# A hold and a pin for the conditioning passes around the column change of the first down product

## The chip, the cores and the metric

The kernel runs on one core of one Trainium2 chip. The metric is the device time of one execution in microseconds (us). A core has five engines with a queue of instructions each: PE (matmuls, with PEld for its weight loads), DVE and ACT (elementwise work), POOL, and SP, which here only issues DMAs. Each engine takes its own instructions in the order in which they stand, and an instruction waits there until the semaphores that it needs have been raised by other engines or by a landed DMA.

## What is computed

One layer of a decoder at batch 1, 256 positions and width 2048, all in fp32. Nine vectors of 2048 numbers, the conditioning, come from one vector `c`:

```python
mod = (silu(c) @ w_ada + b_ada).reshape(b, 9, 2048)
h = modulate(rms_norm(x, norm_ffn1), mod[0], mod[1])
x = x + 0.5 * mod[2] * swiglu(h, w_ffn1_gu, w_ffn1_down)     # DFF = 5632
h = modulate(rms_norm(x, norm_mix), mod[3], mod[4])
x = x + mod[5] * token_mixing(h, w_in, w_ret_branch, w_swa_branch, w_out, sinks)
h = modulate(rms_norm(x, norm_ffn2), mod[6], mod[7])
x = x + 0.5 * mod[8] * swiglu(h, w_ffn2_gu, w_ffn2_down)
return rms_norm(x, norm_final)
```

`w_ada` has 2048 x 18432 numbers. It is applied to a single row, so the kernel does that product on DVE, not on PE.

## The kernel before

**Matmuls in three parts.** A product in fp32 precision is made of three passes in the faster format fp32r. Each operand is split in a high part (a cast) and a low part (what the cast lost); then high by high, low by high and high by low are added up in PSUM (lines 338, 339 and 341 in `products`). A weight tile `raw` is 128 x 4 x 512 numbers, 1 MB, and comes in by one DMA from SP (`load`, line 328). It is used in two halves; a **half step** is one of them: ACT casts the high part `wh` (line 351), DVE subtracts to get the low part `wl` (line 353), and PE runs 12 matmuls, two k blocks by two row tiles by three. The left operand of a down product, the activations, is split in the same way on ACT and DVE (`a`, lines 386 and 387). There are four buffers for `raw`, and three each for `wh` and `wl`.

**The down product** (`down_product`) multiplies the 256 x 5632 activations with `w_ffn1_down`, 2048 columns wide. It does columns 0 to 1023 first: 11 blocks of k, each a `gemm_part` with two weight tiles, so four half steps a block. The results of the four PSUM banks are then multiplied with the gate row and added to `x` on DVE (`add_gated`, lines 607 and 608), with a sum of squares on ACT (line 536). Then columns 1024 to 2047 follow into the same four banks: seven blocks in the same way, and the last four in an order written out by hand. Going from the first two column groups to the last two is the **column change**.

**The conditioning passes.** While the first feed-forward part runs, the vectors 2, 4 and 3 of the conditioning are made beside it. A row tile of `w_ada` (128 x 2048, 1 MB) is loaded by SP (`ada_load`, line 201) and reduced against `silu(c)` on DVE in four passes of 512 columns (`ada_pass`, line 206; in the trace each is a pass and a short read of its sum). The generator `conditioning` yields after each pass. `tick` is called after each half step; it adds `rate` to a count and takes one pass for each whole number reached. When it takes a pass, the generator first issues the load of the row tile after the next boundary (`ahead`, four passes on). The row tiles live in two places, halves of one `slot` tile (`two_rows`), so the load of a row tile waits until the last pass of the row tile two before it is done.

**What sets the order.** SP's queue stands in the order in which the program is written. The orders of PE, DVE and ACT are made by the scheduler of the framework, which may pull an instruction ahead of its place in the program; `tc.issue_after(x)` forbids that it goes ahead of `x`. `low[-1]` is the newest low part made by `split`. Only the last part of a down product has an order written out by hand.

Of the kernel before, what the change touches and what calls it, by code (L numbers as in the profile page):

```python
# [21 lines left out]
NT = S // P  # L22
KD = D // P
KF = DFF // P
CH = 512
KB = 4
# [51 lines left out]
def layer_kernel(  # L78
# [40 lines left out]
    def nm(s):  # L119
        uid[0] += 1  # L120
        return f"{s}_{uid[0]}"

    def acc_bank():
        return psa.tile([P, CH], F32, tag="acc", name=nm("pa"))
# [70 lines left out]
    AQ = 4  # L195

    def ada_load(m, k, w, loads=1):
        src = w_ada[(m * KD + k) * P : (m * KD + k + 1) * P, :]
        for i in range(loads):
            at = slice(i * D // loads, (i + 1) * D // loads)  # L200
            nc.sync.dma_start(w[:, at], src[:, at])

    def ada_pass(k, w, sums, q, passes=AQ):

        at = slice(q * D // passes, (q + 1) * D // passes)
        nc.vector.tensor_tensor_reduce(  # L206
            out=w[:, at],
            in0=w[:, at],
            in1=cact[:, at],
            scale=1.0,  # L210
            scalar=0.0,
            op0=ALU.mult,
            op1=ALU.add,
            accum_out=sums[:, k, q : q + 1],
        )

    def ada_sums():
        return two.tile([P, KD, AQ], F32, tag="sums", name=nm("sums"))

    def ada_end(m, ks, sums, i=None, passes=AQ):  # L220

        dest = modc[:, m, ks]
        nc.vector.tensor_reduce(out=dest, in_=sums[:, ks, :passes], axis=AX.X, op=ALU.add)
        nc.vector.tensor_add(dest, dest, bcols[:, m, ks])
        if i is not None:
            nc.vector.tensor_mul(dest, dest, gains[:, i, ks])
# [16 lines left out]
    def conditioning(outputs, place, behind):  # L243


        tiles = [(m, k) for m, _, _ in outputs for k in range(KD)]
        held = {}
        step = 0
        for m, gain, row in outputs:
            sums = ada_sums()  # L250
            for k in range(KD):
                for q in range(AQ):
                    for i in range(step // AQ, min((step + pace["ahead"]) // AQ + 1, len(tiles))):
                        if i not in held:
                            held[i] = place()
                            ada_load(*tiles[i], held[i])
                    if behind is not None and step < 2 * AQ:
                        with tc.issue_after(behind.ins):
                            ada_pass(k, held[step // AQ], sums, q)
                    else:  # L260
                        ada_pass(k, held[step // AQ], sums, q)
                    step += 1
                    if k == KD - 1 and q == AQ - 1:
                        ada_end(m, slice(0, KD), sums, gain)
                        if row is not None:
                            gate_out(m, row)
                    yield
# [15 lines left out]
        return nc.gpsimd.dma_start(row, gate_d[m // 3][None, :].broadcast_to([P, D]))  # L283


    pace = {"steps": iter(()), "rate": 0.0, "due": 0.0, "behind": None}

    def set_pace(outputs, halves, place, ahead):
        assert next(pace["steps"], None) is None
# [3 lines left out]
        pace["ahead"] = ahead  # L293

    def tick():
        pace["due"] += pace["rate"]
        while pace["due"] >= 1.0:
            pace["due"] -= 1.0
            next(pace["steps"], None)
# [16 lines left out]
    def step():  # L316

        while side:
            try:
                next(side[0])  # L320
                break
            except StopIteration:
                side.pop(0)
# [33 lines left out]
    cast, low, newest = [], [], []  # L357
# [32 lines left out]
    def gemm_part(act, w, col0s, banks, kb, KT, ahead=None):  # L390

        pairs = [act.pair(kb * 2 + h) for h in range(2)]
        for i, c0 in enumerate(col0s):
            raw = None if ahead else load(w, kb, c0)
            for h in range(2):
                if ahead:
                    wh, wl = ahead[h]
                else:
                    wh, wl = split(wsp, "w", raw[:, 2 * h : 2 * h + 2, :], CH)
                ah, al = pairs[h]  # L400
                products(
                    banks[i], ah, al, wh, wl, kb + h == 0, kb * KB + 2 * h + 2 == KT
                )
                tick()
            turn_step()

    def gemm(act, w, col0s, KT=KD, ahead=None):
        banks = [[acc_bank() for _ in range(NT)] for _ in col0s]
        for kb in range(KT // KB):
            gemm_part(act, w, col0s, banks, kb, KT, None if kb else ahead)  # L410
            step()
        return banks
# [286 lines left out]
    def down_product(act, w, gate, KT, spare, before, after):  # L699


        ssq = small(NT * 4, "ssq")
        banks = gemm(act, w, [0, CH], KT=KT)
        for i in range(2):
            for t in range(NT):
                add_gated(banks[i][t], t, i * CH, gate, ssq)
        c0s = [2 * CH, 3 * CH]
        banks = [[acc_bank() for _ in range(NT)] for _ in c0s]
        nb = KT // KB
        for kb in range(nb - 4):  # L710
            gemm_part(act, w, c0s, banks, kb, KT)
        with tc.manual_schedule(engines=ORDERED):
            a, b = nb - 2, nb - 1
            home = home_tile().rearrange("p i (h n) -> p (i h) n", h=2)
            pairs, late = {}, {}

            def place(kb, h):
                if kb >= a:
                    halves = home[:, (kb - a) * 2 + h].rearrange("p (i n) -> p i n", i=2)
                    return [halves[:, i] for i in range(2)]  # L720
                if kb == a - 1:
                    return None
                return [back.tile([P, CH], F32R, tag="back", name=nm("back")) for _ in range(2)]

            for kb in (a - 2, a - 1, a, b):
                wt = weight(w, kb, c0s[0])
                pairs[kb] = []
                for h in range(2):
                    pairs[kb].append(act.pair(kb * 2 + h, place(kb, h)))
                    products(  # L730
                        banks[0], *pairs[kb][h], *wt(h), kb + h == 0, kb == b and h == 1
                    )
                n = {a - 2: a - 2, a - 1: a, a: b, b: a - 1}[kb]
                wt = weight(
                    w, n, c0s[1], spare if n == a - 2 else None if n < a else home_views()
                )
                late[n] = [(n, h, wt(h)) for h in range(2)]
            steps = [step for kb in (a - 2, a, a - 1, b) for step in late[kb]]

            def last(t, which):  # L740
                for kb, h, (wh, wl) in which:
                    products(
                        banks[1], *pairs[kb][h], wh, wl, kb + h == 0, kb == b and h == 1, [t]
                    )

            last(0, steps)
            before()
            root_table()
            for t in range(NT):
                add_gated(banks[0][t], t, c0s[0], gate, ssq)  # L750
            c0, y = c0s[1], {}

            def gated(t):
                y[t] = t512()
                nc.vector.tensor_mul(y[t], banks[1][t], gate[:, c0 : c0 + CH])

            def added(t):
                xs = x_sb[:, t, c0 : c0 + CH]
                nc.vector.tensor_add(xs, xs, y[t])

            def squared(t):
                square_sum(
                    ssq[:, t * 4 + 3 : t * 4 + 4], x_sb[:, t, c0 : c0 + CH], flat_tile
                )

            after(
                [Root(ssq, t) for t in range(NT)],
                (gated, added, squared),
                [lambda i=i: last(1, steps[i : i + 1]) for i in range(8)],
            )  # L770
# [113 lines left out]
    held = Held()  # L884
# [5 lines left out]
    behind = [[back.tile([P, CH], F32, tag="back", name=nm("back")) for _ in range(NT)] for _ in range(2)]  # L890
# [15 lines left out]
    def place(m, k):  # L906
        if k < 1:
            rows_of[m, k] = raw_row()
        else:
            ring.append(ring.pop(0))  # L910
            rows_of[m, k] = ring[-1]
        ada_load(m, k, rows_of[m, k], 2 if k < 2 else 1)
# [45 lines left out]
    banks, moved = {}, set()  # L958
# [50 lines left out]
    for g, ks in enumerate(groups):  # L1009
# [5 lines left out]
        due = 0 if final else 2 * len(groups[g + 1])  # L1015
# [21 lines left out]
    gate = gate_row()  # L1037
    tiles.append(slot())
    row_ring.append(two_rows())
    pace["rate"] = (192 - 32) / 117  # L1040
    pace["ahead"] = AQ
    ffn_up(held, gu, tiles, EARLY, turned=range(EARLY, DFF // CH))
    gate_in = gate_load(gate, 2)
# [317 lines left out]
    for p in range(2):  # L1361
        sg = first if p == 0 else gates(p)
        c0s = [(2 * p + i) * CH for i in range(2)]
        for g, a, w in ((1, a_swa, w_swa_branch), (0, a_ret, w_ret_branch)):
            assert g == 1 or not turns
            banks = gemm(a, w[0], c0s)
# [139 lines left out]
```

## Time and profile before

| what | us |
|---|---|
| median of three runs | 2375.23 (2373.46 to 2377.26) |
| the profiled execution's own time | 2376.93 |
| its span, first to last instruction | 2375.2 |
| PE busy | 2342.6 |
| DVE busy | 1702.5 |
| ACT busy | 1322.7 |
| first `add_gated` of the first down product starts at | 638.2 |

Times inside the trace are counted from the start of the span. "Busy" means that an instruction of the engine runs. A matmul is shown for its whole latency, and matmuls overlap, so PE can be busy without a break while each matmul's own share is shorter than its duration; the distance between starts tells the rate. In a list of instructions the columns are start and duration in us, engine, line, operation, output<-inputs, shape and count; square brackets give the engine's idle time before it and who ended that. In a table of windows each engine has its busy time and the number of its instructions, then come the granted PE clock as a share of full speed, the DMA share and GB/s. In a list of waits the three numbers are the total, how often, and the longest.

### The profile page before, as it was taken

The page shows a single profiled execution, that of the slowest core. Times are in us where ns is not written, and L with a number is a line of the kernel's source. Part 1 is how long each engine was busy: PE and PEld are TensorE (multiplying, and loading weights), DVE is VectorE, ACT ScalarE, POOL GpSimd, SP SyncE. Part 2 cuts the span into 40 slices and gives each one's busy share as a digit, 9 for nine tenths or more (in the row PEclk, how much of TensorE's full clock was granted, in tenths as well). Part 3 has the DMA queues.
Part 4 walks back from the last instruction along what each step waited for, and adds up shares of the span by engine and source line. Part 5 has one row for each costly group of instructions (what it writes and reads, how often), then busy time and mean ns, then how long its engine had stood idle before and what let it go on. Part 6 is the DMA issues. An engine that isn't in the chain of part 4 may idle for free.

```text
span 2375.2 us, 28320 instructions
## 1 busy us (share of the span) xinstructions
PE 2342.6 (99%) x10438; PEld 1921.9 (81%) x10438; DVE 1702.5 (72%) x2635; ACT 1322.7 (56%) x1816; POOL 7.7 (0%) x18
## 2 busy tenths in 40 slices
PE   7999999999999999999999999999999999999998
PEld 5788888888788887778888888887888888888886
DVE  6887799788977768976777776677555555555656
ACT  6543456555446568775556564466445455455544
POOL 0000000000000000000000000000000000000000
PEclk9999999999999999999999999999999999999999
DMA  9977789998876787986778887755677777766553
GB/s 358 362 279 274 269 279 355 373 343 315 313 264 242 272 276 237 245 241 237 273 259 298 298 301 279 286 200 184 244 242 240 253 241 254 247 220 204 190 200 124
DMA packets 186028, 627.87 MB, mean 264 GB/s; under 512 B 108769, under 2 KB 109153, under 8 KB 115361
## 3 DMA queue, kind: packets, MB, share of 16 engines
q1 hardware_dynamic: 183810, 615.21, 74.4%
q0 software_dynamic: 1504, 9.81, 1.0%
q8 instruction: 82, 1.34, 0.2%
q10 hardware_dynamic: 576, 1.05, 0.1%
q14 instruction: 56, 0.46, 0.1%
HBM read 597.16 MB, written 4.22 MB: 253 GB/s over the span
## 4 chain that ended last, share of the span: by engine, by line
PE 94%; DVE 2%; DMA 2%; issue 1%; ACT 0%; SPq 0%; DVEq 0%; ACTq 0%
PE pa L341 31%; PE pa L338 31%; PE pa L339 31%; DMA raw<-in_w_ada_dram 1%; DVE wl L353 1%; PE ps L1201 0%; DMA x_sb<-in_x_dram 0%; DVE raw L206 0%; PE pd L1117 0%; DMA raw<-in_w_ffn_gu_dram 0%; DVE slot L206 0%; ACT wh L351 0%; PE ps L817 0%; DVE t L607 0%; PE ps L1117 0%
## 5 line engine op out<-in xcount | busy, mean ns | idle before, releaser
L353 DVE TENSOR_TENSOR wl<-raw,wh 128x1024 fp32r<-128x1024 f32 x794 | 964.6, 1222 | 532.9 <-ACT wh L351 531.1
L351 ACT CAST wh<-raw 128x1024 fp32r<-128x1024 f32 x794 | 833.5, 1053 | 906.1 <-PE pa L339 876.2
L338 PE MATMUL pa<-wh,hh 128*128 128x512 f32 x2192 | 856.4, 392 | 3.3 <-ACT wh L351 3.3
L339 PE MATMUL pa<-wh,hl 128*128 128x512 f32 x2192 | 855.2, 390 | 0.2 <-DVE hl L601 0.2
L341 PE MATMUL pa<-wl,hh 128*128 128x512 f32 x2192 | 779.4, 392 | 1.4 <-DVE wl L353 1.2
L338 PEld LDWEIGHTS pa<-wh,hh 128*128 128x128 f32 x2192 | 411.9, 188 | 92.3 <-ACT wh L351 5.3
L341 PEld LDWEIGHTS pa<-wl,hh 128*128 128x128 f32 x2192 | 410.5, 188 | 90.0 <-DVE wl L353 4.1
L339 PEld LDWEIGHTS pa<-wh,hl 128*128 128x128 f32 x2192 | 412.3, 188 | 85.2 <-DVE hl L601 0.4
L339 PE MATMUL pa<-wh,a 128*128 128x512 f32 x944 | 367.3, 391 | 0.0
L341 PE MATMUL pa<-wl,a 128*128 128x512 f32 x944 | 349.6, 391 | 3.1 <-DVE wl L353 3.1
L338 PE MATMUL pa<-wh,a 128*128 128x512 f32 x944 | 350.6, 391 | 0.0
L206 DVE CUSTOM_DVE_ANT_0 slot<-slot,cact 128x512 f32<-128x512 f32 (+1 forms) x280 | 210.3, 800 | 12.5 <-DMA slot<-in_w_ada_dram 12.5
L341 PEld LDWEIGHTS pa<-wl,a 128*128 128x128 f32 x944 | 177.7, 188 | 40.7 <-DVE wl L353 4.2
L339 PEld LDWEIGHTS pa<-wh,a 128*128 128x128 f32 x944 | 177.6, 188 | 38.4 <-DVE a L387 1.5
L338 PEld LDWEIGHTS pa<-wh,a 128*128 128x128 f32 x944 | 177.6, 188 | 37.0 <-ACT a L386 0.4
L512 ACT COPY slot<-back 128x512 uint16<-128x512 uint16 x140 | 93.4, 766 | 0.0
L206 DVE CUSTOM_DVE_ANT_0 raw<-raw,cact 128x512 f32<-128x512 f32 (+1 forms) x108 | 70.7, 706 | 21.2 <-DMA raw<-in_w_ada_dram 14.9
L206 DVE CUSTOM_DVE_ANT_0 rows_x<-rows_x,cact 128x512 f32<-128x512 f32 x124 | 78.7, 687 | 9.7 <-DMA rows_x<-in_w_ada_dram 9.3
L387 DVE TENSOR_TENSOR a<-slot,a 128x512 fp32r<-128x512 f32 x118 | 80.6, 684 | 0.3
L496 ACT COPY flat<-t 128x512 uint16<-128x512 uint16 x128 | 72.7, 617 | 3.0 <-DVE t L1274 2.6
L386 ACT CAST a<-slot 128x512 fp32r<-128x512 f32 x118 | 72.6, 616 | 0.0
L206 DVE DVE_READ_ACCUMULATOR2_ANT sums<- 128x1 f32 x512 | 42.0, 82 | 0.0
(206 smaller groups left out, 1162.5 us busy)
## 6 DMA issues: line engine op xcount, KB each, us to landing
raw<-in_w_ffn_gu_dram SPq DMA_DIRECT2D x160, 1024.0 KB, 5.2
raw<-in_w_in_dram SPq DMA_DIRECT2D x104, 1024.0 KB, 5.5
raw<-in_w_ffn_down_dram SPq DMA_DIRECT2D x88, 1024.0 KB, 4.8
slot<-in_w_ada_dram SPq DMA_DIRECT2D x83, 1024.0 KB, 7.2
rows_x<-in_w_ada_dram SPq DMA_DIRECT2D x31, 1024.0 KB, 7.4
raw<-in_w_ada_dram SPq DMA_DIRECT2D x26, 1024.0 KB, 5.5
raw<-in_w_ffn_gu_dram SPq DMA_DIRECT2D x32, 512.0 KB, 5.8
raw<-in_w_swa_branch_dram SPq DMA_DIRECT2D x16, 1024.0 KB, 6.0
```

Of the source, the lines that this page charges most:

```text
L206: nc.vector.tensor_tensor_reduce(out=w[:, at], in0=w[:, at], in1=cact[:, at], scale=1.0, scalar=0.0, op0=ALU.mult, op1=ALU.add, accum_out= ...
L338: nc.tensor.matmul(ps, ah[:, j, ts], wh[:, j, :], start=first, stop=False)
L339: nc.tensor.matmul(ps, al[:, j, ts], wh[:, j, :], start=False, stop=False)
L341: nc.tensor.matmul(ps, ah[:, j, ts], wl[:, j, :], start=False, stop=last).ins
L351: cast.append(nc.scalar.copy(hi, src).ins)
L353: low.append(nc.vector.tensor_sub(lo, src, hi.bitcast(F32)).ins)
L386: nc.scalar.copy(hi, v)
L387: nc.vector.tensor_sub(lo, v, hi.bitcast(F32))
L496: nc.scalar.copy(planes[:, i, :], words(src)[:, :, i])
L512: nc.scalar.copy(into[:, :, :, i], held["turned"][:, i])
```

## The change

Three things are changed.

- For eight half steps, the last block of columns 0 to 1023 and the first block of columns 1024 to 2047, `tick` returns at once: no conditioning pass is taken (`hold`).
- After the hold, `pin` counts down from twelve, one per half step. While it isn't zero, each pass is written behind the newest low part, `tc.issue_after(low[-1])`. The count goes down ahead of the passes of the same half step, so eleven half steps have such passes.
- The rate of passes goes from 160 in 117 half steps to 160 in 109, from 1.368 to 1.468 a half step, from the start of the pacing after the eighth feed-forward chunk on.

The loop of `gemm` is written out in `down_product`, since the hold is set inside it; its work is the same.

```diff
                     if behind is not None and step < 2 * AQ:
                         with tc.issue_after(behind.ins):
                             ada_pass(k, held[step // AQ], sums, q)
+                    elif pace["pin"]:
+                        with tc.issue_after(low[-1]):
+                            ada_pass(k, held[step // AQ], sums, q)
                     else:
                         ada_pass(k, held[step // AQ], sums, q)
...
     def tick():
+        if pace["hold"]:
+            pace["hold"] -= 1
+            return
+        pace["pin"] = max(0, pace["pin"] - 1)
         pace["due"] += pace["rate"]
...
-        banks = gemm(act, w, [0, CH], KT=KT)
+        nb = KT // KB
+        banks = [[acc_bank() for _ in range(NT)] for _ in range(2)]
+        for kb in range(nb):
+            if kb == nb - 1 and KT == KF:
+                pace["hold"], pace["pin"] = HOLD, 12
+            gemm_part(act, w, [0, CH], banks, kb, KT)
+            step()
...
+    HOLD = 8
-    pace["rate"] = (192 - 32) / 117
+    pace["rate"] = (192 - 32) / (117 - HOLD)
```

Three places in the queues show what this moves. In all of them `slot_603` is the pair of places for row tiles of `w_ada`, the numbers behind `raw`, `wh`, `wl` and `a` name single tiles, and line numbers of the changed kernel are higher by 7 from `tick` on (353 is 360, 387 is 394, 607 and 608 are 614 and 615).

**First place: DVE at the column change.** `raw_922` is the second weight tile of columns 1024 and up. Before:

```order
L607 TENSOR_TENSOR t_909_5037<-pa_765_4110,row_601_3114 128x512
L206 ISA slot_603_3116,sums_840_4598<-slot_603_3116,cact_103 128x512
L206 ISA sums_840_4598 128x1
...
L353 TENSOR_TENSOR wl_924_5092<-raw_922_5089,wh_923_5091 128x1024
L387 TENSOR_TENSOR a_916_5049<-slot_12_129,a_916_5049 128x512
L608 TENSOR_TENSOR x_sb_97<-x_sb_97,t_907_5032 128x512
L608 TENSOR_TENSOR x_sb_97<-x_sb_97,t_909_5037 128x512
L353 TENSOR_TENSOR wl_926_5110<-raw_922_5089,wh_925_5109 128x1024
```

The three left-out pairs of rows are passes too: four passes stand between the last gate product and the low part `wl_924`. Now:

```order
L614 TENSOR_TENSOR t_909_5042<-pa_765_4116,row_601_3114 128x512
L360 TENSOR_TENSOR wl_924_5094<-raw_922_5091,wh_923_5093 128x1024
L394 TENSOR_TENSOR a_916_5054<-slot_12_129,a_916_5054 128x512
L615 TENSOR_TENSOR x_sb_97<-x_sb_97,t_907_5037 128x512
L615 TENSOR_TENSOR x_sb_97<-x_sb_97,t_909_5042 128x512
L360 TENSOR_TENSOR wl_926_5110<-raw_922_5091,wh_925_5109 128x1024
L360 TENSOR_TENSOR wl_931_5134<-raw_929_5131,wh_930_5133 128x1024
L206 ISA slot_603_3116,sums_828_4520<-slot_603_3116,cact_103 128x512
```

No pass stands there any more; the next is behind `wl_931`, and so on.

**Second place: SP from the column change on.** SP's loads of weight tiles and of row tiles, before:

```order
L328 DMA raw_922_5089<-in_w_ffn1_down_dram 128x2048
L201 DMA slot_603_3116<-in_w_ada_dram 128x2048
L328 DMA raw_929_5133<-in_w_ffn1_down_dram 128x2048
L201 DMA slot_603_3116<-in_w_ada_dram 128x2048
L328 DMA raw_934_5171<-in_w_ffn1_down_dram 128x2048
L328 DMA raw_941_5213<-in_w_ffn1_down_dram 128x2048
L201 DMA slot_603_3116<-in_w_ada_dram 128x2048
L328 DMA raw_946_5251<-in_w_ffn1_down_dram 128x2048
L201 DMA slot_603_3116<-in_w_ada_dram 128x2048
L328 DMA raw_953_5295<-in_w_ffn1_down_dram 128x2048
L328 DMA raw_958_5331<-in_w_ffn1_down_dram 128x2048
```

and now:

```order
L335 DMA raw_922_5091<-in_w_ffn1_down_dram 128x2048
L335 DMA raw_929_5131<-in_w_ffn1_down_dram 128x2048
L335 DMA raw_934_5168<-in_w_ffn1_down_dram 128x2048
L201 DMA slot_603_3116<-in_w_ada_dram 128x2048
L335 DMA raw_941_5212<-in_w_ffn1_down_dram 128x2048
L201 DMA slot_603_3116<-in_w_ada_dram 128x2048
L335 DMA raw_946_5249<-in_w_ffn1_down_dram 128x2048
L335 DMA raw_953_5292<-in_w_ffn1_down_dram 128x2048
L201 DMA slot_603_3116<-in_w_ada_dram 128x2048
L335 DMA raw_958_5330<-in_w_ffn1_down_dram 128x2048
```

The loads of row tiles have moved behind `raw_934`. What they wait for stands on DVE, whose rows for `raw_934` and `raw_941` were

```order
L353 TENSOR_TENSOR wl_936_5174<-raw_934_5171,wh_935_5173 128x1024
L387 TENSOR_TENSOR a_928_5130<-slot_12_129,a_928_5130 128x512
L206 ISA slot_603_3116,sums_840_4598<-slot_603_3116,cact_103 128x512
L206 ISA sums_840_4598 128x1
...
L353 TENSOR_TENSOR wl_938_5191<-raw_934_5171,wh_937_5190 128x1024
L353 TENSOR_TENSOR wl_943_5216<-raw_941_5213,wh_942_5215 128x1024
```

with four passes in one piece, and are

```order
L360 TENSOR_TENSOR wl_933_5151<-raw_929_5131,wh_932_5150 128x1024
L206 ISA slot_603_3116,sums_828_4520<-slot_603_3116,cact_103 128x512
...
L360 TENSOR_TENSOR wl_936_5171<-raw_934_5168,wh_935_5170 128x1024
L206 ISA slot_603_3116,sums_828_4520<-slot_603_3116,cact_103 128x512
...
L360 TENSOR_TENSOR wl_938_5189<-raw_934_5168,wh_937_5188 128x1024
L206 ISA slot_603_3116,sums_828_4520<-slot_603_3116,cact_103 128x512
...
L360 TENSOR_TENSOR wl_943_5215<-raw_941_5212,wh_942_5214 128x1024
L206 ISA slot_603_3116,sums_828_4520<-slot_603_3116,cact_103 128x512
```

with one or two passes behind each low part and none ahead of it.

**Third place: the start of the down product, on ACT and PE.** `a_779` and `a_780` are the first two pairs of activations, `raw_781` and `raw_787` the first weight tiles. ACT before:

```order
L386 CAST a_779_4199<-slot_12_129 128x512
L351 CAST wh_788_4247<-raw_787_4245 128x1024
L386 CAST a_780_4202<-slot_12_129 128x512
L351 CAST wh_790_4265<-raw_787_4245 128x1024
L351 CAST wh_795_4290<-raw_794_4288 128x1024
```

ACT now:

```order
L393 CAST a_779_4205<-slot_12_129 128x512
L393 CAST a_780_4208<-slot_12_129 128x512
L358 CAST wh_788_4254<-raw_787_4252 128x1024
L358 CAST wh_790_4271<-raw_787_4252 128x1024
L358 CAST wh_795_4298<-raw_794_4296 128x1024
```

The cast `wh_788` has gone behind `a_780`. PE's first matmuls of the product were

```order
L338 MATMUL pa_762_4107<-wh_782_4207,a_779_4199 128x512
L338 MATMUL pa_763_4108<-wh_782_4207,a_779_4199 128x512
L339 MATMUL pa_762_4107<-wh_782_4207,a_779_4199 128x512
L341 MATMUL pa_762_4107<-wl_783_4208,a_779_4199 128x512
L339 MATMUL pa_763_4108<-wh_782_4207,a_779_4199 128x512
```

and are

```order
L345 MATMUL pa_762_4113<-wh_782_4213,a_779_4205 128x512
L345 MATMUL pa_763_4114<-wh_782_4213,a_779_4205 128x512
L345 MATMUL pa_764_4115<-wh_788_4254,a_779_4205 128x512
L345 MATMUL pa_765_4116<-wh_788_4254,a_779_4205 128x512
L346 MATMUL pa_762_4113<-wh_782_4213,a_779_4205 128x512
```

The first use of `wh_788` was the thirteenth matmul of the product and is the third.

More of the change, by code (lines that the diff above doesn't have):

```diff
@@ L283, in gate_load @@
         return nc.gpsimd.dma_start(row, gate_d[m // 3][None, :].broadcast_to([P, D]))
-    pace = {"steps": iter(()), "rate": 0.0, "due": 0.0, "behind": None}
+    pace = {"steps": iter(()), "rate": 0.0, "due": 0.0, "behind": None, "hold": 0, "pin": 0}
     def set_pace(outputs, halves, place, ahead):
@@ L708, in down_product @@
         banks = [[acc_bank() for _ in range(NT)] for _ in c0s]
-        nb = KT // KB
         for kb in range(nb - 4):
```

## The prediction

> **What bounds the kernel now.** I read the page first, then the table of windows around the column change, then the instructions of PE, DVE and ACT there in order of time, then SP's waits. Busy time and chain say that PE is the bound:
>
> ```profile
> PE 2342.6 (99%) x10438; PEld 1921.9 (81%) x10438; DVE 1702.5 (72%) x2635; ACT 1322.7 (56%) x1816; POOL 7.7 (0%) x18
> PE 94%; DVE 2%; DMA 2%; issue 1%; ACT 0%; SPq 0%; DVEq 0%; ACTq 0%
> ```
>
> So time moves only where PE stops or slows down. Between 480 and 800 us PE's list of waits has one row, and the windows show where it is:
>
> ```profile
> PE pa L341 <- DVE wl L353: 2.4, 1, 2.4
> 630.00:640.00 10.00, 10.00 (x46) 8.26 (x45) 9.34 (x17) 4.27 (x6) 0.00 (x0) 1.00 0.81 316
> 640.00:650.00 10.00, 7.57 (x27) 5.85 (x26) 10.00 (x19) 5.21 (x12) 0.00 (x0) 0.84 0.56 211
> 646.00:650.00 4.00, 3.38 (x8) 2.71 (x9) 4.00 (x6) 1.43 (x5) 0.00 (x0) 0.59 0.27 113
> 482.79 0.45 PE pa L341 x2
> 485.51 0.45 PE pa L341 x2
> ```
>
> The last two rows, of the chain, are the same place in two successive half steps: 12 matmuls in 485.51 - 482.79 = 2.72 us, 0.227 each. From 640 to 650 PE starts 27 matmuls where 46 fit; 19 x 0.227 = 4.3 us are lost. In order of time, PE, then DVE and ACT:
>
> ```profile
> 643.80 0.39 PE L339 MATMUL pa<-wh,a 128*128 128x512 f32 x1
> 646.62 1.12 PE L341 MATMUL pa<-wl,a 128*128 128x512 f32 x2 [2.44 <-DVE wl L353]
> 647.54 0.63 PE L338 MATMUL pa<-wh,a 128*128 128x512 f32 x1
> 647.97 0.63 PE L339 MATMUL pa<-wh,a 128*128 128x512 f32 x1
> 650.61 0.39 PE L339 MATMUL pa<-wh,a 128*128 128x512 f32 x1
> 642.90 0.68 DVE L206 CUSTOM_DVE_ANT_0 slot<-slot,cact 128x512 f32<-128x512 f32 x1
> 643.51 0.69 DVE L206 CUSTOM_DVE_ANT_0 slot<-slot,cact 128x512 f32<-128x512 f32 x1
> ...
> 645.35 1.22 DVE L353 TENSOR_TENSOR wl<-raw,wh 128x1024 fp32r<-128x1024 f32 x1
> 642.69 1.06 ACT L351 CAST wh<-raw 128x1024 fp32r<-128x1024 f32 x1 [0.58 <-PE pa L339]
> ```
>
> The high part is ready at 642.69 + 1.06 = 643.75, but DVE does four passes from 642.90 to 645.35 ahead of the low part. PE stands for 2.44 us, and then starts at 0.43 us instead of 0.227 until about 650; the granted clock of 0.59 over those 4 us is 1.6 us lost. Together that is the 4.3.
>
> **The hold.** In the new order no pass stands between the last gate product and `wl_924`. The low part would start when its high part is ready, about 643.8, and end by 645.1. PE's wait goes, and with it the slow clock: **-4.3** (at least -2.4 if only the wait went). No work is removed: all 192 passes remain, 0.69 us each, and 160 of them still fall between the two rate lines. Eight half steps of 2.72 us have none; the others take 1.468 instead of 1.368, 0.1 x 0.61 us (643.51 - 642.90, the distance of two passes) more of DVE in each 2.72, covered by idle DVE (the row 630 to 640 has 0.66 idle, and it's among the fullest). The gate row and the modulation columns keep their places in the program or come earlier, and POOL's order is the same: nothing.
>
> **The pin.** Here a load is the price. The pass itself is 0.69 us on a DVE that has room. But who waits for it? SP does, for the row tile two ahead goes into the place that this row tile leaves. Before, the scheduler was free to pull passes ahead as soon as their row tile had landed, so this wait was over when SP came to it. Where the four passes stand in one piece, SP issues the row tile 0.38 us behind a weight tile, and the only rows of SP's waits from 640 to 700 us are those of weight tiles:
>
> ```profile
> SPq L328 <- DVE wl L353: 51.8, 10, 8.0
> SPq L328 <- DVE modc L224: 5.6, 1, 5.6
> 649.54 0.33 SPq L328 DMA_DIRECT2D raw<-in_w_ffn_down_dram  x1
> 649.92 0.42 SPq L201 DMA_DIRECT2D slot<-in_w_ada_dram  x1
> raw<-in_w_ffn_down_dram SPq DMA_DIRECT2D x11, 1024.0 KB, 4.9
> slot<-in_w_ada_dram SPq DMA_DIRECT2D x5, 1024.0 KB, 6.8
> L353 DVE TENSOR_TENSOR wl<-raw,wh 128x1024 fp32r<-128x1024 f32 x36 | 43.9, 1223 | 16.4 <-ACT wh L351 16.2
> L206 DVE CUSTOM_DVE_ANT_0 slot<-slot,cact 128x512 f32<-128x512 f32 x44 | 27.9, 686 | 0.0
> L351 ACT CAST wh<-raw 128x1024 fp32r<-128x1024 f32 x36 | 38.0, 1055 | 49.0 <-PE pa L339 49.0
> ```
>
> With the pin a pass can't run before the low part of its half step. SP's load of the row tile thus stands until DVE has reached that half step, and the weight tiles behind it in SP's queue stand too, though their buffers are free. SP's lead of up to four weight tiles is gone. After release the cycle is: row tile issued 0.42, weight tile issued 0.33; of two loads issued together the second lands after 6.8 (the row of the 5 row tiles, all second ones; the first alone takes 4.9); high part 1.06; low part 1.22; then one or two passes, 0.6 to 1.3; and the next row tile is released. That is 0.4 + 6.8 + 1.06 + 1.22 + 1.0 = 10.5 us a row tile. PE needs four passes' worth of half steps for it, 4 / 1.468 x 2.72 = 7.4 us. So each row tile under the pin costs up to 3.1 us. Eleven half steps with 1.468 passes are 16 passes, four row tiles: 4 x 3.1 = 12.4 us without cover. The cover is what is loaded when SP first stands still: in the new order that is `raw_929` and `raw_934`, of which PE still has one or two half steps to go at the release, 2.7 to 5.4 us. Idle PE: 12.4 less 2.7 to 5.4, 7 to 9.7; I take **+9**, near the upper end, since SP comes out of it with a heap of loads that must land one after another. Bounds: 0, if the stock covers all of it (first rival), and 12.4.
>
> These 9 us come in about three waits of 2 to 4 us. What a wait costs beyond itself has two rows: 2.44 us brought the slow clock (above), and 0.86 us didn't:
>
> ```profile
> 377.71 0.73 PE L341 MATMUL pa<-wl,hh 128*128 128x512 f32 x2 [0.86 <-DVE wl L353]
> 378.00:382.00 4.00, 4.00 (x19) 3.25 (x19) 4.00 (x6) 1.05 (x1) 0.00 (x0) 1.00 1.03 426
> ```
>
> I count the slow clock for two of the three, nearer to the 2.44 row, 2 x 1.6 = **+3.2** (0 to 3 x 1.8 = 5.4, with 1.8 as what 4.3 leaves above the 2.44). [...]
>
> **The order at the start of the product.** Nothing in the diff names it, but the rate moves the scheduler. ACT and PE before:
>
> ```profile
> 529.95 0.62 ACT L386 CAST a<-slot 128x512 fp32r<-128x512 f32 x1
> 530.65 1.05 ACT L351 CAST wh<-raw 128x1024 fp32r<-128x1024 f32 x1
> 531.60 0.62 ACT L386 CAST a<-slot 128x512 fp32r<-128x512 f32 x1
> 530.68 0.68 PE L338 MATMUL pa<-wh,a 128*128 128x512 f32 x2
> 531.35 0.51 PE L339 MATMUL pa<-wh,a 128*128 128x512 f32 x1
> ```
>
> Now `a_780` goes ahead of `wh_788`: the cast would start about 530.65 + 0.6 = 531.25 and end at 532.3, while PE wants it at its third matmul, 530.68 + 2 x 0.227 = 531.1. A wait of **+1.2** (0.3, the present loss there, to 1.5). Such small swaps, and the heap of loads at the end of the pin, may happen at a place or two more: **+1.5** (0 to 4).
>
> **Sum.** -4.3 + 9 + 3.2 + 1.2 + 1.5 = +10.6. The profiled execution took 2376.9, its span 2375.2; the median of the runs is 2375.2, 1.7 lower. 2376.9 + 10.6 = 2387.5; from the median it is 2385.8. The clock is my softest term and errs upward if short waits pay too, so I say **2387.5**.
>
> **Rivals.** (1) The stock covers it: not slower. Four buffers of 5.44 us each are 21.8 us of PE work; if the row tile is released 8.3 us (0.4 + 6.8 + 1.06) ahead of PE's need, no weight tile is late. For it speaks that no wait of SP has cost PE anything in the stretch ahead, where PE is never idle:
>
> ```profile
> 500.00:638.00 138.00, 138.00 (x609) 113.75 (x608) 118.28 (x222) 71.76 (x85) 0.00 (x0) 1.00 0.91 332
> ```
>
> Against it: SP's lead is lost once at the hold, where no row tile is released for eight half steps = 21.8 us, exactly the stock, and isn't won back at 10.5 against 7.4. Then -4.3 + 1.2: about 2372 to 2374, within 0.2%. Chance 0.07. (2) No cover at all and the slow clock after every wait, short ones too: -4.3 + 12.4 + 5.4 + 1.5 + 4 = +19, 2394 to 2396. For it: the slow clock shifts nothing that SP waits for. Chance 0.13. (3) The hold doesn't do its work: DVE is still late at the column change, since the gate products and sums (four and four, 0.6 us each) stay there; then the 4.3 remain and it is 2392. Against it: between `wl_921` and `wl_924` now stand four of them, 2.4 us, and no longer four and four passes, 4.9 us. Chance 0.04. The forecast, the lead lost and partly covered: 0.76.
>
> **Range and chances.** From half the idle time under the pin with one slow clock, -4.3 + 4.5 + 1.6 + 1.2 + 1.5 = +4.5, which is 2381.4 from the profiled execution and 2379.7 from the median, so 2380.5, to the second rival, 2395.5; that leaves out the first rival and the ends. A measurement of this kernel can hardly tell less than 0.2% (4.75 us) from no change. Slower by more than that needs over 2380: 0.76 + 0.13 + 0.04 less 0.02 for a weak forecast case, 0.91. Within: 0.07 for the first rival and those 0.02, less 0.01: 0.08. Faster by over 0.2% needs more than the whole stall of 4.3 back: 0.01.
>
> **What will show it.** Right: no PE wait for `wl` near 645; SP waiting for `sums` at line 201 between 630 and 700, several us at a time; PE waits for ACT's `wh` (which stands for a late weight tile) between 660 and 715, with the clock under 1 behind them; a short wait near 532. Wrong: weight tiles issued early in that stretch although row tiles wait, or passes that run ahead of their low part.

## The result and the profile after

The changed kernel took 2389.4 us as a median, the kernel before in the same runs 2376.1. The median counts one execution in a slow state (3723 us, at a granted clock of 0.60), which the ratio leaves out: the other three took 2386.6, 2388.9 and 2389.9 us. The ratio is 1.005 with a 95% interval of 1.0036 to 1.0064: slower by 8.6 to 15 us. The profiled execution took 2389.91 us, with a span of 2387.8.

On the page of the profile, PE is still 94% of the chain. Of the 12.6 us that the span has gained, 8.0 are more idle time of PE (40.6 us, where it was 32.6) and 4.6 more busy time for the same 10438 matmuls. DVE and ACT do the same work as before, and the DMAs move the same 627.87 MB:

```profile
PE 2347.2 (98%) x10438; PEld 1922.7 (81%) x10438; DVE 1702.7 (71%) x2635; ACT 1323.1 (55%) x1816; POOL 7.7 (0%) x18
PE 94%; DMA 2%; DVE 1%; ACT 1%; issue 1%; SPq 0%; DVEq 0%; ACTq 0%
```

Where it went is seen in the same three windows of both kernels: the first part of the down product with the end of the feed-forward part, the column change, and what follows. Before:

```profile
638.00:660.00 22.00, 19.57 (x80) 15.71 (x79) 20.72 (x41) 10.71 (x18) 0.00 (x0) 0.92 0.71 268
660.00:740.00 80.00, 80.00 (x355) 66.31 (x354) 61.02 (x81) 45.35 (x53) 0.00 (x0) 1.00 0.74 269
```

After:

```profile
500.00:638.00 138.00, 136.40 (x601) 112.17 (x600) 111.92 (x202) 71.14 (x85) 0.00 (x0) 1.00 0.88 326
638.00:660.00 22.00, 22.00 (x99) 18.22 (x98) 19.43 (x29) 13.06 (x20) 0.00 (x0) 1.00 0.28 95
660.00:740.00 80.00, 71.89 (x295) 57.60 (x294) 56.59 (x97) 36.59 (x43) 0.00 (x0) 0.94 0.72 277
```

At the column change PE now starts 99 matmuls and no longer 80: 19 x 0.227 = 4.3 us won. In the window behind it, it starts 295 and no longer 355: 60 x 0.227 = 13.6 us lost. In the first window 8 are missing, 1.8 us. On balance 13.6 + 1.8 - 4.3 = 11.1 us are lost.

The win first. On DVE no pass stands at the column change any more; the low part (line 360) follows the gate products:

```profile
645.13 1.28 DVE L614 TENSOR_TENSOR t<-pa,row 128x512 f32<-128x512 f32 x2
646.33 1.21 DVE L360 TENSOR_TENSOR wl<-raw,wh 128x1024 fp32r<-128x1024 f32 x1
```

The loss, from its end to its cause. PE's waits between 640 and 740 us, and the two long ones in order of time, each with the matmul ahead of it and the first one back at full rate:

```profile
PE pa L345 <- ACT wh L358: 7.9, 3, 3.5
PE pa L346 <- DVE a L394: 0.2, 1, 0.2
670.95 0.39 PE L348 MATMUL pa<-wl,a 128*128 128x512 f32 x1
674.86 0.79 PE L345 MATMUL pa<-wh,a 128*128 128x512 f32 x1 [3.53 <-ACT wh L358]
680.46 0.39 PE L346 MATMUL pa<-wh,a 128*128 128x512 f32 x1
694.15 0.39 PE L348 MATMUL pa<-wl,a 128*128 128x512 f32 x1
697.73 0.80 PE L345 MATMUL pa<-wh,a 128*128 128x512 f32 x1 [3.19 <-ACT wh L358]
700.84 0.39 PE L346 MATMUL pa<-wh,a 128*128 128x512 f32 x1
```

PE waits for the high part; ACT, which makes it, waits for the weight tile:

```profile
673.77 1.99 ACT L358 CAST wh<-raw 128x1024 fp32r<-128x1024 f32 x2 [7.40 <-DMA raw<-in_w_ffn_down_dram]
```

And SP, which asks for the weight tile, waits for conditioning passes (`sums`). Its waits from 640 to 720 us, then its issues in order of time, with the row tiles in line 201 and the weight tiles in line 335; the row of DVE (line 206) ends the pass that the second row tile waited for, itself behind a low part:

```profile
SPq L201 <- DVE sums L206: 50.6, 5, 17.7
SPq L335 <- DVE wl L360: 17.2, 4, 6.1
655.93 0.33 SPq L201 DMA_DIRECT2D slot<-in_w_ada_dram  x1
656.36 0.37 SPq L335 DMA_DIRECT2D raw<-in_w_ffn_down_dram  x1
666.28 0.08 DVE L206 DVE_READ_ACCUMULATOR2_ANT sums<- 128x1 f32 x1
666.39 0.33 SPq L201 DMA_DIRECT2D slot<-in_w_ada_dram  x1
666.82 0.86 SPq L335 DMA_DIRECT2D raw<-in_w_ffn_down_dram  x2
679.07 0.33 SPq L201 DMA_DIRECT2D slot<-in_w_ada_dram  x1
679.49 0.38 SPq L335 DMA_DIRECT2D raw<-in_w_ffn_down_dram  x1
689.37 0.33 SPq L201 DMA_DIRECT2D slot<-in_w_ada_dram  x1
689.79 0.38 SPq L335 DMA_DIRECT2D raw<-in_w_ffn_down_dram  x1
```

Each weight tile comes 0.4 us behind a row tile, and the row tiles come 10.5, 12.7 and 10.3 us apart. From the weight tile's issue at 666.82 to the cast at 673.77 are 6.95 us.

Each of the two long waits comes with the slow clock; three windows of 4 us from their ends on:

```profile
674.00:678.00 4.00, 3.14 (x7) 2.48 (x8) 3.16 (x6) 2.80 (x3) 0.00 (x0) 0.50 0.37 154
678.00:682.00 4.00, 4.00 (x14) 3.19 (x13) 4.00 (x9) 1.57 (x2) 0.00 (x0) 0.71 0.51 143
696.00:700.00 4.00, 2.27 (x5) 1.84 (x6) 3.59 (x8) 1.99 (x2) 0.00 (x0) 0.67 1.02 430
```

### The profile page after: what moved, and what is told of

Its sections match the earlier page's. It is cut to its first block, busy times and chain, and to the rows that moved or that the text cites. A ratio compares the mean times of both kernels' runs of the same rounds, so it can differ in the third digit from the quotient of the medians.

```text
span 2387.8 us, 28339 instructions
## 1 busy us (share of the span) xinstructions
PE 2347.2 (98%) x10438; PEld 1922.7 (81%) x10438; DVE 1702.7 (71%) x2635; ACT 1323.1 (55%) x1816; POOL 7.7 (0%) x18
## 2 busy tenths in 40 slices
DMA packets 186028, 627.87 MB, mean 263 GB/s; under 512 B 108769, under 2 KB 109153, under 8 KB 115361
## 4 chain that ended last, share of the span: by engine, by line
PE 94%; DMA 2%; DVE 1%; ACT 1%; issue 1%; SPq 0%; DVEq 0%; ACTq 0%
PE pa L348 31%; PE pa L345 31%; PE pa L346 31%; DMA raw<-in_w_ffn_down_dram 1%; ACT wh L358 1%; DVE wl L360 1%; PE ps L1214 0%; DMA x_sb<-in_x_dram 0%; DMA raw<-in_w_ada_dram 0%; DMA raw<-in_w_ffn_gu_dram 0%; PE pd L1130 0%; DVE slot L206 0%; PE ps L829 0%; SPq L201 0%; PE ps L486 0%
```

## The experiments

The theory, S: a row tile's load stands in SP's queue until a pinned pass is done, and weight tiles stand behind it. Its rivals: H, the hold alone loses SP's lead, since no row tile is released for eight half steps; D, the pinned passes are themselves in the way on DVE.

The runs' times differ by 2 to 6 us among executions of one kernel, much of it outside the down product: PE's 100th matmul starts at 45.6 to 47.7 us in the nine profiles, although PE, DVE, ACT and SP have the same order up to there (it first differs at 402 us). So beside the ratio stands the time from PE's 2000th to its 3100th recorded matmul, which is the stretch from about 477 to 731 us; all the kernels have the same number of them. Each ratio is against the kernel before in runs on the same chip, whose median was 2376.1 to 2376.6 us.

| kernel | median us | ratio to before (95% interval) | stretch us | to before |
|---|---|---|---|---|
| before | 2376.1 | | 254.1 | |
| the change | 2389.4 | 1.005 (1.0036 to 1.0064) | 265.1 | +11.0 |
| hold and rate, no pin | 2376.9 | 1.0001 (0.9992 to 1.001) | 252.4 | -1.7 |
| pin alone | 2386.3 | 1.0038 (1.0023 to 1.0053) | 261.5 | +7.4 |
| rate alone | 2376.0 | 1.0 (0.9991 to 1.001) | 252.8 | -1.3 |
| the change, row tiles by POOL | 2379.1 | 1.0012 (1.0002 to 1.0022) | 256.2 | +2.1 |
| the change, pin on an older low part | 2376.4 | 0.9998 (0.9989 to 1.0007) | 252.6 | -1.5 |
| the change, five half steps with a pin | 2385.3 | 1.0037 (1.0023 to 1.0051) | 261.3 | +7.2 |
| two rates, pin on an older low part | 2375.5 | 0.9992 (0.9983 to 1.0001) | 251.2 | -2.9 |

**Without the pin.** Hold and rate stay:

```diff
-                pace["hold"], pace["pin"] = HOLD, 12
+                pace["hold"] = HOLD
```

> The hold and the higher rate stay, the pin goes. Theory S (row tiles of w_ada stand in SP's queue until a pinned pass is done, and weight tiles stand behind them): without the pin the scheduler may pull passes ahead again, so the loss of 13 us between 660 and 715 us goes; the stall of 4.3 us at the column change is gone too, and the small waits at the start of the product (2 us) stay. 2373 to 2377 us, same as before or up to 0.1% under it. Theory H (the hold alone empties SP's lead, since no row tile is released for eight half steps): the waits for late weight tiles after 655 us stay, 2383 to 2390 us.

2376.9 us, no difference from before. Of the same windows the last two are

```profile
638.00:660.00 22.00, 21.45 (x95) 17.45 (x94) 20.69 (x37) 12.45 (x20) 0.00 (x0) 1.00 0.72 270
660.00:740.00 80.00, 80.00 (x355) 66.24 (x354) 63.08 (x88) 46.38 (x54) 0.00 (x0) 1.00 0.77 288
```

All 355 matmuls are back behind 660, and SP's waits for passes from 640 to 720 us come to one:

```profile
SPq L201 <- DVE sums L206: 2.0, 1, 2.0
```

So the hold, at this rate, doesn't cost SP its lead, and H falls. The pin costs 11.0 + 1.7 = 12.7 us in the stretch.

**The pin alone.** The same half steps are pinned, at the rate of before and with no hold:

```diff
-        if pace["hold"]:
-            pace["hold"] -= 1
-            return
+        if pace["wait"]:
+            pace["wait"] -= 1
+            if not pace["wait"]:
+                pace["pin"] = 12
...
-                pace["hold"], pace["pin"] = HOLD, 12
+                pace["wait"] = HOLD + 1
...
-    pace["rate"] = (192 - 32) / (117 - HOLD)
+    pace["rate"] = (192 - 32) / 117
```

> The pin stays on the same half steps, the hold and the higher rate go (1.368 passes a half step). Theory S: row tiles are still released only when DVE reaches the half step, so SP waits for sums several times for some us each, and PE loses 6 to 12 us between 650 and 715 us; a cycle of 10.5 us against 4 / 1.368 x 2.72 = 8.0 us costs a little less a row tile than in the full change. 2380 to 2388 us. Theory H: without the hold no lead is lost, 2376 us as before.

2386.3 us, and the same picture without a hold. SP's waits from 640 to 720 us and PE's from 640 to 740:

```profile
SPq L201 <- DVE sums L206: 53.7, 6, 18.4
PE pa L346 <- ACT wh L359: 4.5, 2, 3.8
PE pa L347 <- DVE a L395: 2.6, 2, 1.8
```

The longest of SP's waits is 18.4 us, where it was 17.7 in the change: the first pinned row tile holds SP up for so long with or without a hold. Here D has a share: the 2.6 us for `a` are two waits for DVE. Ahead of the longer one DVE had stood for 4.47 us, until 657.48, for a late high part, and then did five pinned passes among four low parts before it came to the activations:

```profile
657.48 1.23 DVE L361 TENSOR_TENSOR wl<-raw,wh 128x1024 fp32r<-128x1024 f32 x1 [4.47 <-ACT wh L359]
665.09 1.28 DVE L395 TENSOR_TENSOR a<-slot,a 128x512 fp32r<-128x512 f32 x2
665.83 0.50 PE L347 MATMUL pa<-wh,a 128*128 128x512 f32 x1 [1.79 <-DVE a L395]
```

The stall at the column change is gone in this run too, though no half step is held: PE has no wait between 640 and 657 us.

**Row tiles by POOL.** The passes and their pin stay, but SP's queue is spared:

```diff
-            nc.sync.dma_start(w[:, at], src[:, at])
+            queue = nc.gpsimd if pace["pin"] else nc.sync
+            queue.dma_start(w[:, at], src[:, at])
```

> The full change, but the row tiles of w_ada that are asked for while the pin is on are loaded by POOL's queue and no longer by SP's; the passes stay where they are. Theory S: weight tiles no longer stand behind row tiles, so PE's waits for the high part wh between 660 and 715 us fall from 8 us to under 3 and most of the 13 us come back: 2376 to 2381 us. Theory D (the pinned passes themselves are in the way on DVE, ahead of low parts and activations): nothing comes back, 2386 to 2392 us.

Of the 11.0 us in the stretch 8.9 come back, and PE has no wait for `wh` behind 640 us any more. One wait is left:

```profile
689.87 0.50 PE L347 MATMUL pa<-wh,a 128*128 128x512 f32 x1 [2.71 <-DVE a L395]
685.54 0.69 DVE L207 CUSTOM_DVE_ANT_0 slot<-slot,cact 128x512 f32<-128x512 f32 x1 [3.82 <-DMA slot<-in_w_ada_dram]
```

DVE stands for 3.82 us at a pass whose row tile hasn't landed, does four passes, and only then the low parts. So D has a share here as well, by a row tile that is itself late. In the changed kernel PE's waits for DVE are 0.2 us. DVE waits there for one row tile between 640 and 720 us, at 694.16, and PE's wait for the late weight tile (694.54 to 697.73) covers it:

```profile
694.16 0.69 DVE L206 CUSTOM_DVE_ANT_0 slot<-slot,cact 128x512 f32<-128x512 f32 x1 [0.95 <-DMA slot<-in_w_ada_dram]
```

**The pin on an older low part.** Passes, half steps and queues stay; only the low part behind which a pass stands is that of two half steps earlier:

```diff
-                        with tc.issue_after(low[-1]):
+                        with tc.issue_after(low[-3]):
                             ada_pass(k, held[step // AQ], sums, q)
...
-        del low[:-1]
+        del low[:-3]
```

> The full change, but each pinned pass is put behind the low part of two half steps earlier and no longer behind the newest. The number of passes and the half steps with a pin stay. Theory S: SP gets the release up to two half steps, 5.4 us, earlier, and the cycle of 10.5 us a row tile comes under the 7.4 us of PE work: the waits after 660 us go nearly all, 2373 to 2378 us. Theory D: the same passes fill DVE in the same stretch, so the loss stays, 2385 to 2391 us.

2376.4 us: the loss is gone, with PE's waits from 640 to 740 us at

```profile
PE pa L345 <- ACT wh L358: 0.5, 1, 0.5
```

SP still waits for passes, up to 14.1 us at a time, but its issues come earlier and closer:

```profile
650.58 0.33 SPq L201 DMA_DIRECT2D slot<-in_w_ada_dram  x1
657.04 0.33 SPq L201 DMA_DIRECT2D slot<-in_w_ada_dram  x1
664.67 0.33 SPq L201 DMA_DIRECT2D slot<-in_w_ada_dram  x1
672.13 0.33 SPq L201 DMA_DIRECT2D slot<-in_w_ada_dram  x1
```

6.5, 7.6 and 7.5 us apart, near the 7.4 us of PE work that four passes stand for. So it isn't SP's wait as such that costs. What fits both kernels is the cycle from one row tile's release to the next, which costs when it is longer than the work that it brings.

**Half the pin.** Five half steps have pinned passes and no longer eleven:

```diff
-                pace["hold"], pace["pin"] = HOLD, 12
+                pace["hold"], pace["pin"] = HOLD, 6
```

> The full change with the pin's count at 6 and no longer 12: five half steps with pinned passes, 7.3 passes, about two row tiles and no longer four. Theory S: the price goes with the row tiles under the pin, so about half of the 13 us between 660 and 715 us is left, 2380 to 2385 us. Rival: SP's lead is lost once, at the hold and the first pinned row tile, and all of the loss follows from that: 2387 to 2390 us, as in the full change.

2385.3 us, 0.3 above the one range and below the other. Against the kernel without a pin the stretch loses 261.3 - 252.4 = 8.9 us, where eleven half steps lose 12.7. Half of the pin has 70% of the price, so the price doesn't go with the number of row tiles: the first wait, with its slow clock, is most of it.

```profile
671.91 0.80 PE L345 MATMUL pa<-wh,a 128*128 128x512 f32 x1 [3.67 <-ACT wh L358]
668.00:672.00 4.00, 0.33 (x3) 0.09 (x1) 2.65 (x9) 1.19 (x2) 0.00 (x0) 0.85 1.01 426
672.00:676.00 4.00, 4.00 (x10) 3.14 (x11) 3.73 (x4) 1.85 (x2) 0.00 (x0) 0.50 1.01 426
```

**The rate alone.** Hold and pin go, the rate of 1.468 stays:

```diff
-                pace["hold"], pace["pin"] = HOLD, 12
+                pass
```

> Only the higher rate of 1.468 passes a half step stays; hold and pin go. If the two short waits at the start of the down product (1.4 and 0.7 us lost near 532 and 544 us in the changed kernel) come from the rate's effect on the scheduler, they are here too; if they come from the hold or the pin, they are not. Theory S: no waits for late weight tiles after 655 us. The stall of 4.3 us at the column change is the open point: it stays if only the hold removes it, and the time is then 2378 to 2380 us; it shrinks if the passes merely have to stand elsewhere at that place, and then 2374 to 2378 us.

2376.0 us, in the lower of the two ranges. The two short waits at the start of the product are here (near 531 and 543 us; 1.5 and 0.7 us lost), and the two kernels that keep the rate of before up to there don't have them, so they come from the rate. What is new is the column change: the stall is gone without any hold. On DVE

```profile
643.57 1.22 DVE L360 TENSOR_TENSOR wl<-raw,wh 128x1024 fp32r<-128x1024 f32 x1
644.70 0.68 DVE L394 TENSOR_TENSOR a<-slot,a 128x512 fp32r<-128x512 f32 x1
645.30 0.68 DVE L206 CUSTOM_DVE_ANT_0 slot<-slot,cact 128x512 f32<-128x512 f32 x1
```

the four passes stand behind the low part and the activations, ahead of which they stood before. The stall was where the scheduler happened to put one batch of passes, and another rate puts it elsewhere. Not all of the gain is kept: PE has a new wait of 0.91 us near 653.

**A version from the findings.** The rate of before up to the hold (so no swap at the start of the product), a higher one after it, and the older low part:

```diff
-                        with tc.issue_after(low[-1]):
+                        with tc.issue_after(low[-3]):
...
-        del low[:-1]
+        del low[:-3]
...
                 pace["hold"], pace["pin"] = HOLD, 12
+                pace["rate"] = 40 / 23
...
-    pace["rate"] = (192 - 32) / (117 - HOLD)
+    pace["rate"] = (192 - 32) / 117
```

> A version made from the findings: the rate of before (1.368) up to the hold, 40 passes in the 23 half steps behind it (1.74), and each pinned pass behind the low part of two half steps earlier. Theory S: no stall at the column change, no swap at the start of the product, SP's lead kept: 3 to 4 us under before, 2372 to 2374 us. Rival: at 1.74 passes a half step DVE itself becomes late after 655 us (1.74 x 0.61 + 1.14 + 0.3 = 2.5 us of each 2.72), and the gain goes back: 2376 us or more.

From 500 to 740 us PE has one wait left:

```profile
PE pa L346 <- DVE a L394: 0.7, 1, 0.7
```

The stretch is 2.9 us shorter than before, in one profile. The median of 2375.5 us lies in neither range: the stall, the swap and the waits for weight tiles are gone, and the one wait left is for DVE, as the rival has it. The times give 0.9992 with an interval of 0.9983 to 1.0001, so that it is faster isn't shown.

## Why the prediction was right

Forecast were 2387.5 us with 2380.5 to 2395.5; it is 2389.4. The steps below give what is lost in the stretch, from the distances of PE's starts against 0.227 us a matmul:

- **The hold: -4.3.** It came, 19 matmuls at the column change. But the gain isn't the hold's own: the rate alone removes the stall as well, and so does the pin alone.
- **The pin: +9 of idle PE.** The mechanism held at each link, from pass to SP to weight tile to cast to PE. The cycle was worked out as 10.5 us and is 10.5, 12.7 and 10.3. The size was too high: two waits of 3.53 and 3.19 us, 6.7 in all, and not three. Nor is it a price for each row tile, as the five half steps with a pin show.
- **The slow clock: +3.2.** It was two waits, as counted, but more for one of them. From 670.95 to 680.46 are 14 matmuls: 9.51 - 14 x 0.227 = 6.3 us lost, 2.8 more than the wait of 3.53. From 694.15 to 700.84 are 8: 6.69 - 8 x 0.227 = 4.9, 1.7 more than the wait of 3.19. That is 4.5 in all; some 0.3 us of each are lost without a slow clock too, as the third, short wait shows: 1.47 us lost near 711 for a wait of 1.20, at a granted clock of 1.00. So 6.7 and 4.5 stand for 9 and 3.2: 11.2 against 12.2, two errors that partly cancel.
- **The start of the product: +1.2.** 1.5 us are lost there, 1.2 more than the 0.3 of before.
- **A place or two more: +1.5.** 0.73 us near 545 and 1.47 near 711 (PE's third wait, 1.20 us, for a high part whose cast stands right behind that of `a` on ACT), and 0.47 near 684 and 0.17 near 669, together 2.84.

Sum as measured: -4.3 + 6.7 + 4.5 + 1.2 + 2.8 = 10.9; the stretch says 11.0, the forecast 10.6. The path was right, but that the sum is so close is luck: 9 was 2.3 too high, and the slow clock and the small places were 1.3 too low each. The span grew by 12.6; 1.7 of that is the later 100th matmul (47.7 against 46.0), up to which nothing differs.

One step failed though the number held. The argument against the first rival was that "SP's lead is lost once at the hold, where no row tile is released for eight half steps". The run without a pin has the hold and keeps the lead; the run with the pin alone loses it without a hold. It's the pin alone: with it a pass can't run until DVE has come to its half step, so SP can't be ahead of DVE by more than a row tile, though there are four buffers for weight tiles (SP's longest wait for a pass is 17.7 us with the hold and 18.4 without). The first rival fell for that reason.

## What to carry to other kernels

An order that is forced on one engine is forced on all queues that wait for it: before a pass is pinned, look for the DMA that takes its buffer over, and for what stands behind that DMA. What seems to count is the cycle from one release to the next (issue, landing, cast, low part, pass) against the work of the bound engine that it brings; two half steps of slack for the pin turned distances of 10.3 to 12.7 us into 6.5 to 7.6 and took the whole price away. And a stall that a scheduler's choice has made may go with a small change of rate, so try the smallest change first.

## What the runs showed of the hardware

The slow clock doesn't follow the length of a wait smoothly. Waits of 0.86 us (the kernel before, at 377.71), 1.20 (the changed kernel, at 712.00) and 1.79 (the pin alone, at 665.83) brought none: the granted clock is 1.00 from 378 to 382, from 710 to 720 and from 660 to 670 in those runs. The wait of 2.44 us in the kernel before and that of 3.19 in the changed one came with half the clock for 3.41 us each, from 646.75 and from 697.37 on, and the changed kernel's 3.53 with 6.83 us of it, from 673.48 on. For the 3.67 us of the five half steps with a pin and the 3.81 of the pin alone, 6.8 us of it are an estimate from the granted clock: 0.85, 0.50 and 0.80 in the three windows of 4 us from 668 on in the one run, 0.96 and 0.70 in the two of 10 us from 670 on in the other. Both come to 3.4 us of full clock lost, which is 6.8 us at half.

The slow clock doesn't begin at a fixed place of a wait: in the changed kernel it began 1.4 us before the first long wait was over (674.86) and 0.4 us before the end of the second (697.73), in the kernel before 0.1 us behind the end (646.62). So part of it can fall into the wait, where PE starts nothing anyway. By the distances of starts, the waits of 2.44 and 3.19 us cost 1.9 and 1.7 us beyond themselves and that of 3.53 cost 2.8; of that some 0.3 come with a wait that brings no slow clock. What decides, these waits do not show.
